# Up projection of a gated MLP: one pair of K tiles in seven block products, in 1024-column groups

## The chip, the cores and the metric

The kernel runs on one core of one Trainium2 chip. The metric is the device time of one execution in microseconds, the median of several runs of the same program. Beside it there is one profiled execution with its trace.

The engines are named as the profile names them: PE is TensorE (matmul; PEld its weight loads), DVE VectorE, ACT ScalarE, POOL GpSimd, SP the sequencer that issues nearly all transfers.

## The reference

One decoder layer on 256 tokens of width 2048: RMSNorm, a combined projection, mLSTM and forgetting-attention heads, an output projection with a residual, then the gated MLP, then a gated per-layer embedding. The part that matters here is the MLP:

```python
h = rms_norm(x, ffn_norm_g[i])
u = h @ w_up[i]                          # (256, 2048) @ (2048, 2 * 5632)
a, g = jnp.split(u, 2, axis=-1)
a = causal_dwconv(a, conv_w[i], conv_b[i])     # width 3, per column, over the tokens
x = x + (jax.nn.gelu(a, approximate=False) * g) @ w_down[i]
```

All of it is float32. The activations are only drawn from random inputs; sizes are fixed (`SEQ = 256`, `D_MODEL = 2048`, `D_FF = 5632`).

## The kernel before, in words

**Products.** Every large product is made in three matmuls of 128 x 128 by 128 x 512: weights and activations are split into a rounded part `hi` and a rest `lo`, and `hi*hi + hi*lo + lo*hi` is summed in PSUM. The activations are the stationary operand (128 features by 128 tokens) and the weights move. The 256 tokens are two halves, `t = 0, 1`.

**The stream of weights.** `run_stream` (L213) takes a list of steps. A step has weight sources of 512 KB (`srcs`), a `split` and a `fn`. SP loads a source into one of six `raw` buffers (four of `RAW`, two of `RAW_FFN`); a load is issued only once the buffer six loads earlier has been given back, strictly in order. `halves` (L200) splits a raw block: ScalarE casts it to `hi` (L208), VectorE subtracts to get `lo` (L210). There are five hi/lo pairs, and splits are issued four steps ahead of the matmuls: the loop issues the split of step i+4, then the matmuls of step i, and then pulls two pieces of work from side jobs (`pull`, L173).

**What sets the order.** This program order is a priority, not the final order. The tile framework plans the program on a timeline of its own, and on each engine an instruction that is ready there can pass an earlier one that still waits there. On the chip each engine then keeps the planned order.

**Up projection before.** `up(q)` (L1009) for q = 0 to 10 makes 512 columns of `a` and the 512 matching columns of `g`, each by `token_group` (L263): eight steps of two K tiles, twelve matmuls each, into two PSUM banks. At its end `up_evac` (L913) scales each bank on ScalarE into `z` (L918), and VectorE transposes it in 32 x 32 blocks into `sq` (L919). After the last bank the side job `ffn_job(q)` (L925) is queued: sixteen transfers `Y<-sq` (L931) on SP complete the transposition, then come the convolution (ScalarE L951, eight multiply-adds on VectorE L954, the halo on GpSimd), GELU (L962), the product with `g` (L966) and the split into `uT` (L129, L130). For the K pairs listed in `SEVEN`, four sums E3, E5, E6, E7 of the activation's blocks are made as well (L980) and split into `uE`.

**Down projection before.** After q = 5 and after q = 10 `down` (L1079) multiplies the finished part of `u` by `w_down`, in two groups of 1024 columns each, by `quad_group` (L303). A group has four banks D11, D21, D12, D22 (token half, column half). A K tile in plain form (kind "R", 12 matmuls) adds to all four. Some pairs of K tiles are done as a 2 x 2 block product in seven products instead of eight (Strassen, in Winograd's form): step "o1" (two raws loaded, one split whole, 6 matmuls), "o2" (half a raw split, then four adds of weight blocks in place in the two raws, L357; 3 matmuls), "c1" and "c2" (each raw split whole, 6 matmuls each). Three of the seven products go straight into D banks, four into further banks Q1, Q5, Q6 and Q7, so 21 matmuls take the place of 24. The raw buffers of o1 are given back only at c1 and c2. After the last c2 `mid` combines the Q banks; after a D bank's last matmul `end` takes it up. `weave` (L1022) writes the order out by hand: so many plain steps first (`head`), then per pair o1, n//3 plain steps, o2, the rest of n less one, c1, c2 and one more.

**PSUM.** Two tags, `mm` and `aux`, of four banks each. In a quad group the D banks have one and the Q banks the other, changed over from group to group.

Of the kernel before, what the change touches and what calls it, by code (L numbers as in the profile page):

```python
# [9 lines left out]
F32 = mybir.dt.float32  # L10
# [27 lines left out]
QF = 24  # L38
SEVEN = ((3, 5, 7), (13, 15, 17))
PAD = 112  # L40


@with_exitstack
def layer_kernel(
# [858 lines left out]
    with tc.tile_pool(name="ffn", bufs=1) as fp:  # L903
        uT = fp.tile([P, QF, 512], F32R, name="uT")
        uE = fp.tile([P, max(map(len, SEVEN)), 4, 256], F32R, name="uE")
# [5 lines left out]
        sq = {}  # L911

        def up_evac(q, ag):  # L913
            def f(t, b):
                if ag == 0 and t == 0:
                    sq[q] = fp.tile([P, 2, 4, NT, 4, 32], F32, tag="sq", name="sq")
                z = fp.tile([P, 512], F32, tag="z", name="z", bufs=3)
                act.activation(z, b, AF.Copy, scale=rstd2[:, t : t + 1])  # L918
                dve.transpose(sq[q][:, ag, :, t].rearrange("p j f r -> p f j r"),  # L919
                              z.rearrange("p (f j c) -> p f j c", f=4, j=4))  # L920
                if ag == 1 and t == NT - 1:
                    side.append(ffn_job(q))
            return f

        def ffn_job(q):  # L925
# [46 lines left out]
            for p in (2 * q, 2 * q + 1):  # L972
                if p in in_seven:
                    f = 2 * (p % 2)
                    v = u[:, f : f + 2].rearrange("p f t i r -> p f t (i r)")
                    e = cf[:, 0:512].rearrange("p (e s) -> p e s", e=4)
                    a11, a12, a21, a22 = v[:, 0, 0], v[:, 1, 0], v[:, 0, 1], v[:, 1, 1]
                    for dst, p0, p1 in ((e[:, 1], a21, a22), (e[:, 3], a21, a11), (e[:, 2], a11, e[:, 1]),
                                        (e[:, 0], a12, e[:, 2])):
                        dve.tensor_sub(dst, p0, p1)  # L980
                    yield
                    w = uE[:, in_seven[p]].rearrange("p u (e s) -> p u e s", e=2)
                    act.copy(w[:, :, 0], e)
                    dve.tensor_sub(w[:, :, 1], e, f32(w[:, :, 0]))
                    yield
# [20 lines left out]
        blocks = []  # L1006
        x2 = aT["cur"]

        def up(q):  # L1009
            for ag in range(2):  # L1010
                blocks.extend(token_group(w_up, all_k, lambda: x2, ag * FF + q * 512, 512, up_evac(q, ag),
                                          tag=("mm", "aux")[ag]))

        def u_unit(p, name):
            if name[0] == "E":
                v = uE[:, in_seven[p], "3567".index(name[1])]
                return v[:, 0:128], v[:, 128:256]
            t, i = int(name[0]) - 1, int(name[1]) - 1
            v = uT[:, (2 * p + i) % QF]
            return v[:, t * P : (t + 1) * P], v[:, 256 + t * P : 256 + (t + 1) * P]  # L1020
# [10 lines left out]

        def tmp(i):
            return fp.tile([P, 512], F32, tag="z", name=f"t{i}", bufs=3)

        pT = {}

        def load_p():
            pr = tmp(3).rearrange("p (t d) -> p t d", t=NT)
            nc.sync.dma_start(out=pr, in_=p[0, 0].rearrange("(t p) d -> p t d", p=P))
            yield 6  # L1040
# [4 lines left out]
            pT["t"] = fp.tile([P, 2, 512], F32R, tag="c", name="pT")  # L1045
            for k in range(2):
# [3 lines left out]
        def down_mid(c, ends):  # L1050
            def f(st):
                if ends and c == 0:
                    side.append(load_p())
                xc = [[xs[:, t, (c + n) * 512 : (c + n + 1) * 512] for n in range(2)] for t in range(NT)]
# [24 lines left out]
        def down(pairs, seven, ends, order):  # L1079
            for c in (0, 2):  # L1080
# [3 lines left out]
                cols = w_down[0][:, c * 512 : (c + 2) * 512].rearrange("k (h n) -> k h n", h=2)  # L1084
                tags = ("aux", "mm") if (c == 0) == ends else ("mm", "aux")
                grp = quad_group(lambda k, cols=cols: cols[k * P : (k + 1) * P], seq, u_unit, tags, down_mid(c, ends),
                                 down_end(c, ends))
                if c == 0:
                    st = grp[first]
                    st.fn = lambda hi, lo, fn=st.fn: (pull(10 ** 6), fn(hi, lo))  # L1090
                blocks.extend(grp)

        for q in range(6):
# [11 lines left out]
        def gate_done(c0, n):  # L1105
            sg = {}

            def f(t, b, i=0, j=n):
                if "r" not in r3:
                    r3["r"] = rstd_of(ssq3, "ple")  # L1110
                if i == 0:
                    sg[t] = fp.tile([P, 512], F32, tag="z", name="sg", bufs=3)
                w = (j - i) // (2 if i else 1)
# [46 lines left out]
```

## Time and profile before

| | us |
|---|---|
| median of 3 runs | 1254.61 (1253.37 to 1256.06) |
| profiled execution | 1254.04 |
| its span, first to last instruction | 1252.2 |
| PE busy | 1246.1 |
| DVE busy | 808.4 |
| ACT busy | 662.6 |
| mean granted TensorE clock | 1.000 |

The time of an execution holds 1.8 us outside the span. In the profile's groups, a row has the line, engine and operation, the tiles written and read, the shape and the count, then busy time in all, mean ns of one, idle time before them and what ended it. In a timeline row the first number is the start, the second the length, both in us, and the bracket has the engine's idle time before it and what ended it. The stage limits in the text (434.2, 697.2, 802.6, 1020.4, 1147.3 us from the span's start) are the first matmuls of up 0 to 5, the first down, up 6 to 10, the second down and the last stage.

### The profile page before, as it was taken

The page shows a single profiled execution, that of the slowest core. Times are in us where ns is not written, and L with a number is a line of the kernel's source. Part 1 is how long each engine was busy: PE and PEld are TensorE (multiplying, and loading weights), DVE is VectorE, ACT ScalarE, POOL GpSimd, SP SyncE. Part 2 cuts the span into 40 slices and gives each one's busy share as a digit, 9 for nine tenths or more (in the row PEclk, how much of TensorE's full clock was granted, in tenths as well). Part 3 has the DMA queues.
Part 4 walks back from the last instruction along what each step waited for, and adds up shares of the span by engine and source line. Part 5 has one row for each costly group of instructions (what it writes and reads, how often), then busy time and mean ns, then how long its engine had stood idle before and what let it go on. Part 6 is the DMA issues. An engine that isn't in the chain of part 4 may idle for free.

```text
span 1252.2 us, 16051 instructions
## 1 busy us (share of the span) xinstructions
PE 1246.1 (100%) x5699; PEld 1048.7 (84%) x5699; DVE 808.4 (65%) x1044; ACT 662.6 (53%) x918; POOL 35.8 (3%) x90
## 2 busy tenths in 40 slices
PE   9999999999999999999999999999999999999998
PEld 7899988888888888888888888888888888888887
DVE  6455566555565555676576697847577659978554
ACT  7555545445554555555465554445455546556542
POOL 2000000000000000000000000000000000000000
PEclk9999999999999999999999999999999999999999
DMA  8667877864567767677777675767767765787661
GB/s 286 173 180 219 255 237 216 209 180 137 162 185 196 236 222 218 202 224 218 212 223 226 186 241 169 234 190 215 231 200 230 222 193 185 222 217 247 205 210 51
DMA packets 161856, 258.77 MB, mean 207 GB/s; under 512 B 38377, under 2 KB 65905, under 8 KB 161777
## 3 DMA queue, kind: packets, MB, share of 16 engines
q1 hardware_dynamic: 161168, 257.57, 68.9%
q8 instruction: 44, 0.72, 0.2%
q14 instruction: 35, 0.29, 0.1%
q10 hardware_dynamic: 385, 0.16, 0.0%
q0 software_dynamic: 224, 0.03, 0.0%
HBM read 237.76 MB, written 2.12 MB: 192 GB/s over the span
## 4 chain that ended last, share of the span: by engine, by line
PE 99%; DMA 0%; SPq 0%; DVE 0%; ACT 0%; issue 0%; DVEq 0%
PE tg L288 26%; PE tg L289 26%; PE tg L290 26%; PE qgD L324 5%; PE qgD L325 5%; PE qgD L326 5%; PE qgQ L325 1%; PE qgQ L324 1%; PE qgQ L326 1%; PE xT L141 1%; PE mob L752 0%; DMA xs<-in_x_dram 0%; PE sc L633 0%; PE ob L661 0%; PE msc L727 0%; PE pt L654 0%
## 5 line engine op out<-in xcount | busy, mean ns | idle before, releaser
L210 DVE TENSOR_TENSOR lo<-raw,hi 128x1024 fp32r<-128x1024 f32 (+3 forms) x475 | 561.4, 1190 | 370.8 <-ACT hi L208 356.4
L208 ACT CAST hi<-raw 128x1024 fp32r<-128x1024 f32 (+3 forms) x475 | 482.6, 1025 | 455.1 <-PE tg L290 304.7
L288 PE MATMUL tg<-hi,x2T 128*128 128x512 f32 x704 | 274.1, 389 | 0.0
L290 PE MATMUL tg<-hi,x2T 128*128 128x512 f32 x704 | 274.0, 389 | 0.0
L289 PE MATMUL tg<-lo,x2T 128*128 128x512 f32 x704 | 273.9, 389 | 0.0
L288 PE MATMUL tg<-hi,hT 128*128 128x512 f32 (+2 forms) x480 | 181.8, 383 | 0.0
L289 PE MATMUL tg<-lo,hT 128*128 128x512 f32 (+2 forms) x480 | 180.3, 378 | 0.0
L290 PE MATMUL tg<-hi,hT 128*128 128x512 f32 (+2 forms) x480 | 180.2, 379 | 0.0
L289 PEld LDWEIGHTS tg<-lo,x2T 128*128 128x128 f32 x704 | 132.1, 188 | 27.5
L290 PEld LDWEIGHTS tg<-hi,x2T 128*128 128x128 f32 x704 | 132.1, 188 | 27.4
L288 PEld LDWEIGHTS tg<-hi,x2T 128*128 128x128 f32 x704 | 132.1, 188 | 27.3
L325 PE MATMUL qgD<-lo,uT 128*128 128x512 f32 x286 | 111.3, 389 | 0.0
L326 PE MATMUL qgD<-hi,uT 128*128 128x512 f32 x286 | 111.2, 389 | 0.0
L324 PE MATMUL qgD<-hi,uT 128*128 128x512 f32 x286 | 103.6, 389 | 0.0
L290 PEld LDWEIGHTS tg<-hi,hT 128*128 128x128 f32 x480 | 89.9, 188 | 12.7
L289 PEld LDWEIGHTS tg<-lo,hT 128*128 128x128 f32 x480 | 90.2, 188 | 12.2
L288 PEld LDWEIGHTS tg<-hi,hT 128*128 128x128 f32 x480 | 90.0, 188 | 12.0
L326 PEld LDWEIGHTS qgD<-hi,uT 128*128 128x128 f32 x286 | 53.7, 188 | 11.2
L324 PEld LDWEIGHTS qgD<-hi,uT 128*128 128x128 f32 x286 | 53.7, 188 | 11.2
L325 PEld LDWEIGHTS qgD<-lo,uT 128*128 128x128 f32 x286 | 53.7, 188 | 11.0
L289 PE MATMUL tg<-lo,x3T 128*128 128x512 f32 (+1 forms) x144 | 52.7, 366 | 0.0
L288 PE MATMUL tg<-hi,x3T 128*128 128x512 f32 (+1 forms) x144 | 52.7, 367 | 0.0
(227 smaller groups left out, 1093.3 us busy)
## 6 DMA issues: line engine op xcount, KB each, us to landing
raw<-in_w_up_dram SPq DMA_DIRECT2D x176, 512.0 KB, 4.6
raw<-in_w_down_dram SPq DMA_DIRECT2D x88, 512.0 KB, 4.7
raw<-in_w_in_dram SPq DMA_DIRECT2D x79, 512.0 KB, 4.3
raw<-in_w_out_dram SPq DMA_DIRECT2D x32, 512.0 KB, 4.3
raw<-in_w_ple_gate_dram SPq DMA_DIRECT2D x32, 512.0 KB, 4.7
Y<-sq SPq DMA_DIRECT2D x176, 64.0 KB, 3.2
raw<-in_w_in_dram SPq DMA_DIRECT2D x24, 416.0 KB, 3.6
raw<-in_w_in_dram SPq DMA_DIRECT2D x16, 408.0 KB, 3.7
```

Of the source, the lines that this page charges most:

```text
L141: pe.transpose(bk[:, t * P : (t + 1) * P], xs[:, t, k * P : (k + 1) * P], ident)
L208: act.copy(hi[:, :w], raw[:, :w])
L210: dve.tensor_sub(lo[:, :w], raw[:, :w], f32(hi[:, :w]))
L288: pe.matmul(bk[:, : e - c], ah, h[:, i, c:e], start=first, stop=False)
L289: pe.matmul(bk[:, : e - c], ah, l[:, i, c:e], start=False, stop=False)
L290: pe.matmul(bk[:, : e - c], al, h[:, i, c:e], start=False, stop=last)
L324: pe.matmul(st[bk], ah, hi[:, cols], start=first, stop=False)
L325: pe.matmul(st[bk], ah, lo[:, cols], start=False, stop=False)
L326: pe.matmul(st[bk], al, hi[:, cols], start=False, stop=final)
```

## The change

For q = 1 to 10 the two 512-column groups become one `quad_group` of 1024 columns (columns of `a` and of `g` are the two column halves), with D banks for token half and a/g. One K pair, pair 0 (`S_UP`), is done in seven products, the other seven pairs in plain form; the order is four plain steps, o1, one plain, o2, three plain, c1, c2 and six plain. Group 0 stays as it was. Pair 0's activation sums are made once, by the side job `x2_sums` in group 0, on VectorE, and split into `x2E`.

`up_mid` combines the Q banks into four SBUF tiles t11 to t22, scaled by the token's RMS factor: two reads of Q1 on ScalarE, four sums on VectorE, three scalings on ScalarE. `up_end` replaces the ScalarE evacuation of each bank by one VectorE instruction, bank x factor + tile, and the transposition follows as before.

Room is found elsewhere: the convolution's tile `c` now lies in the second half of `sq`, the E sums of the downs are kept in ten places (E3 of a pair takes the place of that pair's block 21, which seven products don't read; pair 7, which is also used in plain form, has its own), and four temporaries `t0` to `t3` replace the three buffers `z`. The second down's second group has five plain steps first instead of four, p is loaded at the start of the second down, and PSUM tags alternate through one counter.

```diff
+ONCE = (7,)
+S_UP = (0,)
+UP_ORDER = (4, (5,))
...
+        def x2_sums():
+            for i, p in enumerate(S_UP):
+                a = tmp(0).rearrange("p (k s) -> p k s", k=2)
+                e = tmp(1).rearrange("p (e s) -> p e s", e=4)
+                x = x2[:, 2 * p : 2 * p + 2, :]
+                dve.tensor_add(a, f32(x[:, :, 0:256]), f32(x[:, :, 256:512]))
+                a11, a12, a21, a22 = a[:, 0, 0:128], a[:, 1, 0:128], a[:, 0, 128:256], a[:, 1, 128:256]
+                for dst, p0, p1 in ((e[:, 1], a21, a22), (e[:, 3], a21, a11), (e[:, 2], a11, e[:, 1]),
+                                    (e[:, 0], a12, e[:, 2])):
+                    dve.tensor_sub(dst, p0, p1)
+                yield
+                h = x2E[:, i].rearrange("p u (e s) -> p u e s", e=2)
+                act.copy(h[:, :, 0], e)
+                dve.tensor_sub(h[:, :, 1], e, f32(h[:, :, 0]))
+                yield
...
+        def up_mid(q):
+            def f(st):
+                t11, t12, t21, t22 = (tmp(i) for i in range(4))
+                act.copy(t22, st["Q1"])
+                act.activation(t11, st["Q1"], AF.Copy, scale=rstd2[:, 0:1])
+                dve.tensor_sub(t21, st["Q6"], t22)
+                dve.tensor_add(t12, st["Q5"], t21)
+                dve.tensor_add(t21, st["Q7"], t21)
+                dve.tensor_add(t22, st["Q7"], t12)
+                for v, r in ((t12, rstd2[:, 0:1]), (t21, nr[:, 1:2]), (t22, rstd2[:, 1:2])):
+                    act.activation(v, v, AF.Copy, scale=r)
+                comb[q] = (t11, t12), (t21, t22)
+            return f
+
+        def up_end(q):
+            def f(t, ag, b):
...
+                z = comb[q][t][ag]
+                dve.scalar_tensor_tensor(out=z, in0=b, scalar=rstd2[:, t : t + 1], in1=z, op0=ALU.mult, op1=ALU.add)
+                dve.transpose(sq[q][:, ag, :, t].rearrange("p j f r -> p f j r"),
+                              z.rearrange("p (f j c) -> p f j c", f=4, j=4))
+                if ag == 1 and t == NT - 1:
+                    side.append(ffn_job(q))
+            return f
...
-            c = fp.tile([P, 4, NT, 4, 32], F32, tag="c", name="c")
+            c = T[:, 1].rearrange("p j t f r -> p (j t f r)").rearrange("p (i t f r) -> p i t f r", i=4, t=NT, f=4)
...
         def up(q):
-            for ag in range(2):
-                blocks.extend(token_group(w_up, all_k, lambda: x2, ag * FF + q * 512, 512, up_evac(q, ag),
-                                          tag=("mm", "aux")[ag]))
+            if q == 0:
+                for ag in range(2):
+                    blocks.extend(token_group(w_up, all_k, lambda: x2, ag * FF, 512, up_evac(q, ag),
+                                              tag=("aux", "mm")[ag]))
+                return
+            cols = w_up[0].rearrange("k (h n) -> k h n", h=2)[:, :, q * 512 : (q + 1) * 512]
+            seq = weave([p for p in range(KD // 2) if p not in S_UP], S_UP, *UP_ORDER)
+            blocks.extend(quad_group(lambda k: cols[k * P : (k + 1) * P], seq, x2_unit, tags(), up_mid(q), up_end(q)))
...
-        down(range(10, 22), SEVEN[1], True, ((6, (3, 2, 2)), (4, (3, 3, 3))))
+        down(range(10, 22), SEVEN[1], True, ((6, (3, 2, 2)), (5, (3, 3, 3))))
```

More of the change, by code (lines that the diff above doesn't have):

```diff
@@ new lines, in x2_unit @@
+        def x2_unit(p, name):
+            if name[0] == "E":
+                v = x2E[:, S_UP.index(p), "3567".index(name[1])]
+                return v[:, 0:128], v[:, 128:256]
+            t, k = int(name[0]) - 1, 2 * p + int(name[1]) - 1
+            return x2[:, k, t * P : (t + 1) * P], x2[:, k, 256 + t * P : 256 + (t + 1) * P]
+        nr = sm.tile([P, NT], F32, name="nr")
+        dve.tensor_scalar_mul(nr, rstd2, -1.0)
+        comb = {}
+        def up_mid(q):
[11 more added lines that the diff above has]
+            return f
@@ new lines, in up_end @@
+        def up_end(q):
+            def f(t, ag, b):
+                if t == 0 and ag == 0:
+                    sq[q] = fp.tile([P, 2, 4, NT, 4, 32], F32, tag="sq", name="sq")
+                z = comb[q][t][ag]
[5 more added lines that the diff above has]
+            return f
@@ L981, in ffn_job @@
                     yield
-                    w = uE[:, in_seven[p]].rearrange("p u (e s) -> p u e s", e=2)
-                    act.copy(w[:, :, 0], e)
-                    dve.tensor_sub(w[:, :, 1], e, f32(w[:, :, 0]))
+                    n = 3 * in_seven[p]
+                    w = uE[:, n : n + 3].rearrange("p u (e s) -> p u e s", e=2)
+                    v3 = uE[:, 9] if p in ONCE else uT[:, 2 * p % QF]
+                    v3 = v3.rearrange("p (e s) -> p e s", e=2)[:, :, -128:]
+                    act.copy(w[:, :, 0], e[:, 1:4])
+                    act.copy(v3[:, 0], e[:, 0])
+                    dve.tensor_sub(w[:, :, 1], e[:, 1:4], f32(w[:, :, 0]))
+                    dve.tensor_sub(v3[:, 1], e[:, 0], f32(v3[:, 0]))
                     yield
@@ L1006, in layer_kernel, with tags @@
         blocks = []
[L1007 removed]
+        turns = [0]
+        def tags():
+            turns[0] ^= 1
+            return ("aux", "mm") if turns[0] else ("mm", "aux")
         def up(q):
[L1010 to L1012 removed]
+            if q == 0:
[6 more added lines that the diff above has]
+            blocks.extend(quad_group(lambda k: cols[k * P : (k + 1) * P], seq, x2_unit, tags(), up_mid(q), up_end(q)))
         def u_unit(p, name):
[L1015 to L1016 removed]
+            if name in ("E5", "E6", "E7") or name == "E3" and p in ONCE:
+                v = uE[:, 9 if name == "E3" else 3 * in_seven[p] + "567".index(name[1])]
                 return v[:, 0:128], v[:, 128:256]
[L1018 removed]
+            t, i = (1, 0) if name == "E3" else (int(name[0]) - 1, int(name[1]) - 1)
             v = uT[:, (2 * p + i) % QF]
@@ L1039, in load_p @@
             nc.sync.dma_start(out=pr, in_=p[0, 0].rearrange("(t p) d -> p t d", p=P))
-            yield 6
+            while "bank" not in pT:
+                yield 1
             bk = bank("mm", "pTp")
@@ L1052, in f @@
                 if ends and c == 0:
-                    side.append(load_p())
+                    pT["bank"] = True
                 xc = [[xs[:, t, (c + n) * 512 : (c + n + 1) * 512] for n in range(2)] for t in range(NT)]
@@ L1084, in down @@
                 cols = w_down[0][:, c * 512 : (c + 2) * 512].rearrange("k (h n) -> k h n", h=2)
-                tags = ("aux", "mm") if (c == 0) == ends else ("mm", "aux")
-                grp = quad_group(lambda k, cols=cols: cols[k * P : (k + 1) * P], seq, u_unit, tags, down_mid(c, ends),
+                grp = quad_group(lambda k, cols=cols: cols[k * P : (k + 1) * P], seq, u_unit, tags(), down_mid(c, ends),
                                  down_end(c, ends))
@@ L1090, in down @@
                     st.fn = lambda hi, lo, fn=st.fn: (pull(10 ** 6), fn(hi, lo))
+                    if ends:
+                        grp[0].fn = lambda hi, lo, fn=grp[0].fn: (fn(hi, lo), side.append(load_p()))
                 blocks.extend(grp)
+        side.append(x2_sums())
         for q in range(6):
```

14 lines of the change are left out of this document (8 added, 6 removed).

## The prediction

> **What bounds the kernel now.** I read the page first (busy times, slices, chain), then the waits, then busy time by stage.
>
> ```profile
> span 1252.2 us, 16051 instructions
> PE 1246.1 (100%) x5699; PEld 1048.7 (84%) x5699; DVE 808.4 (65%) x1044; ACT 662.6 (53%) x918; POOL 35.8 (3%) x90
> DVE  6455566555565555676576697847577659978554
> ...
> PE 99%; DMA 0%; SPq 0%; DVE 0%; ACT 0%; issue 0%; DVEq 0%
> ```
>
> TensorE is the whole chain. A busy PE need not be a dense one, so the waits of PE and the distance between starts of matmuls decide (first the waits, then PE's timeline, where the two rows are twelve matmuls apart):
>
> ```profile
> PE warm L81 <- DVE ones L77: 1.1, 1, 1.1
> PE xT L141 <- DMA xs<-in_x_dram: 0.8, 1, 0.8
> ...
> DVE lo L210 <- ACT hi L208: 356.4, 287, 4.6
> ACT hi L208 <- PE tg L290: 304.7, 208, 2.4
> ACT c L951 <- DMA Y<-sq: 19.4, 11, 3.3
> ```
>
> ```profile
> 802.62 0.39 PE L288 MATMUL tg<-hi,x2T 128*128 128x512 f32 x1
> ...
> 805.34 0.39 PE L288 MATMUL tg<-hi,x2T 128*128 128x512 f32 x1
> ```
>
> PE waits 1.9 us in all, both at the start; a 512-column matmul costs 2.72 / 12 = 0.2267 us. ScalarE waits for PE to give back hi/lo buffers and VectorE waits for ScalarE: both follow PE. By stage (up 0-5, first down, up 6-10, second down, then two dense Strassen stretches of the downs):
>
> ```profile
> core 0: us, PE busy (x) PEld busy (x) DVE busy (x) ACT busy (x) POOL busy (x), PEclk, DMA share, GB/s
> 434.20:697.20 263.00, 263.00 (x1169) 217.74 (x1168) 168.51 (x217) 142.61 (x166) 8.32 (x28) 1.00 0.73 219
> 697.20:802.60 105.40, 105.40 (x466) 87.28 (x465) 88.23 (x106) 55.30 (x59) 2.14 (x5) 1.00 0.65 208
> 802.60:1020.40 217.80, 217.80 (x962) 180.35 (x961) 138.42 (x175) 112.92 (x126) 5.93 (x20) 1.00 0.72 214
> 1020.40:1147.30 126.90, 126.90 (x563) 105.02 (x563) 107.78 (x135) 70.74 (x88) 2.08 (x5) 1.00 0.70 211
> 719.00:748.00 29.00, 29.00 (x130) 24.01 (x128) 27.35 (x33) 16.64 (x18) 0.00 (x0) 1.00 0.73 248
> 1046.70:1069.80 23.10, 23.10 (x103) 19.12 (x103) 21.71 (x24) 13.25 (x15) 0.00 (x0) 1.00 0.59 191
> ```
>
> The downs already use seven products for some pairs, in the same code that the change uses for the up projection. The first down has 465 matmuls by the code, and 465 x 0.2267 = 105.4 us, its whole length: nothing is lost there, with VectorE busy 88.23 / 105.40 = 84%, and 94% in the two dense stretches. The clock is 1.00 throughout.
>
> **The change part by part.**
>
> *TensorE, on the path.* A pair of K tiles costs a 1024-column group 24 matmuls in four-product form (2 K tiles x 4 banks x 3) and 21 in seven products. One pair in ten groups: 30 matmuls less, 30 x 0.2267 = **-6.80 us**. A group falls from 192 to 189 matmuls, 42.85 us. Nothing else leaves the path.
>
> The page "TensorE: Matmul & The Clock Gate" of the Trainium skill (section "Wait — 56ns, not 53.3ns?") gives a warm 512-column matmul 215.7 ns from start to start; by it the saving would be 6.5 us. The trace has 226.7 ns for this kernel's matmuls, and the sum goes by the trace.
>
> *VectorE and ScalarE, beside the path.* Prices (groups by form):
>
> ```profile
> L210 DVE TENSOR_TENSOR lo<-raw,hi 128x1024 fp32r<-128x1024 f32 x422 | 513.0, 1221 | 321.0 <-ACT hi L208 306.7 <-DMA Y<-sq 7.5 <-DMA raw<-in_w_in_dram 5.2
> L208 ACT CAST hi<-raw 128x1024 fp32r<-128x1024 f32 x422 | 440.2, 1051 | 414.5 <-PE tg L290 278.4 <-PE qgD L326 47.9 <-DVE raw L357 18.2
> L919 DVE STREAM_TRANSPOSE sq<-z 128x512 f32<-128x512 f32 x44 | 31.1, 707 | 6.6 <-ACT z L918 6.6
> L918 ACT ACTIVATE z<-tg,rstd_ffn 128x512 f32<-128x512 f32 x44 | 30.2, 685 | 14.2 <-PE tg L290 14.2
> L951 ACT ACTIVATE c<-Y,cT 128x256 f32<-128x256 f32 x44 | 22.9, 591 | 19.4 <-DMA Y<-sq 19.4
> L954 DVE SCALAR_TENSOR_TENSOR c<-Y,cT,c 128x248 f32<-128x248 f32 x44 | 20.8, 475 | 11.7 <-ACT c L951 11.5
> L357 DVE TENSOR_TENSOR raw<-raw,raw 128x512 f32<-128x512 f32 x22 | 15.2, 691 | 0.6
> L962 ACT ACTIVATE c<-c 128x1024 f32<-128x1024 f32 x11 | 11.7, 1061 | 3.7 <-DVE c L960 3.6
> L210 DVE TENSOR_TENSOR lo<-raw,hi 128x512 fp32r<-128x512 f32 x13 | 9.0, 693 | 7.5 <-ACT hi L208 7.4
> L208 ACT CAST hi<-raw 128x512 fp32r<-128x512 f32 x13 | 8.1, 621 | 10.9 <-PE qgD L326 5.0 <-DMA raw<-in_w_in_dram 3.2 <-DVE lo L210 1.7
> L1076 DVE TENSOR_TENSOR xs<-qgD,xs 128x512 f32<-128x512 f32 x8 | 5.3, 681 | 1.1 <-PE qgD L326 1.1
> L133 DVE SCALAR_TENSOR_TENSOR x2T<-xT,vT,x2T 128x256 fp32r<-128x256 f32 x8 | 3.5, 477 | 0.6 <-ACT x2T L132 0.6
> L1059 DVE TENSOR_TENSOR t<-qgQ,t 128x512 f32<-128x512 f32 x4 | 2.7, 686 | 0.0
> L1056 ACT COPY t<-qgQ 128x512 f32<-128x512 f32 x4 | 2.3, 574 | 0.0
> ```
>
> VectorE, per group: the Strassen pair is split three times whole and once half instead of twice whole, 1.22 + 0.69, and its weight sums are four adds, 4 x 0.69: +4.67. The middle (Q banks) is four sums, 4 x 0.686: +2.74. The end is four scalar_tensor_tensor of 512 columns with one operand in PSUM, which the trace lacks: not below the plain add's 0.68 (L1076), not above two of 256 columns, 0.95 (L133). I take 0.74, nearer the plain add, since length sets most of it: +2.96. Together +10.4 on 138.42 / 5 = 27.7, so **38.1 of 42.85 us, 89%**. ScalarE loses four evacuations (4 x 0.685) and gets one and a half casts (1.05 + 0.62), a copy and a scaled read of PSUM (0.57 + 0.69) and three scalings out of SBUF of 512 columns, between 0.59 and 1.06 (L951, L962), say 0.75: +2.4 on 22.6, 25.0 of 42.85. All this is priced at nothing on the path; what hides it is the stock of split blocks ahead of PE. With that cover gone each microsecond of VectorE over 42.85 would cost ten, once per group. The dense rows' 94% would carry 38.1 in 40.5 us.
>
> The sums of x2 once, in group 0, some 5 us of VectorE, and the E sums of the downs in four instructions instead of two, lie under the same cover; nothing there.
>
> *The stock, step by step.* There are five hi/lo pairs, so block i+4 is split when PE has finished block i-1, some 10.9 us before its turn (ScalarE's and VectorE's timelines):
>
> ```profile
> 854.50 1.05 ACT L208 CAST hi<-raw 128x1024 fp32r<-128x1024 f32 x1 [1.67 <-PE tg L290]
> ...
> 855.59 1.23 DVE L210 TENSOR_TENSOR lo<-raw,hi 128x1024 fp32r<-128x1024 f32 x1 [1.50 <-ACT hi L208]
> ```
>
> It is done 2.3 us later, so 8.6 us in stock. Let T be the moment PE finishes a group. In the new order (four plain blocks, o1, plain, o2, three plain, c1, c2, six plain) PE starts o1 at T+10.9, o2 at 15.0, c1 at 23.8, c2 at 25.2 and the plain block behind (number 12) at 26.5. VectorE's end is four times 0.74 + 0.71, with one lo between; the first bank closes nine matmuls before T, so from T-1.9 to T+5.1. Behind it stand o1, a plain lo, o2 with its four adds and two more lo: done at 6.3, 7.5, 11.0, 12.2, 13.4, needed at 10.9, 12.2, 15.0 (o2's matmuls), 15.6, 18.4. Smallest stock 3.4 us.
>
> *Two queues the end is moved past.* The sixteen transposing DMAs of the finished group wait at SP for the last transpose. Before (SP, ScalarE):
>
> ```profile
> 847.85 2.51 SPq L931 DMA_DIRECT2D Y<-sq  x4
> ...
> 858.15 2.50 SPq L931 DMA_DIRECT2D Y<-sq  x4
> ...
> 863.34 2.08 ACT L951 ACTIVATE c<-Y,cT 128x256 f32<-128x256 f32 x4 [2.34 <-DMA Y<-sq]
> ```
>
> Group 6 ended at 802.62 + 192 x 0.2267 = 846.1, so Y was there at T+17.2. Afterwards the issue starts at T+5.1 and not T+1.7, but no weight load stands between, since o1 gives no buffer back: 16 x 0.625 = 10 us, plus the 2.7 us that lay between the last issue (860.65) and the landing: T+17.8, say 18. The wait is in ScalarE's queue: behind the convolution (L951) stand the casts, behind these the lo subtractions. GpSimd, 3% busy, waits for the same Y and has nothing else queued.
>
> c1's lo gives back the raw buffer into which SP loads block 12, and every later load is behind that one. The downs have this chain (VectorE: two lo, the first is c1's, ending at 760.98; ScalarE):
>
> ```profile
> 759.75 2.58 DVE L210 TENSOR_TENSOR lo<-raw,hi 128x1024 fp32r<-128x1024 f32 x2 [0.94 <-ACT hi L208]
> ...
> 764.72 1.05 ACT L208 CAST hi<-raw 128x1024 fp32r<-128x1024 f32 x1 [0.92 <-DMA raw<-in_w_down_dram]
> ```
>
> From the end of c1's lo to the dependent cast: 3.74 us. c1's hi/lo buffers come free at T+15.0. If it is split then, its lo ends at T+17.4, block 12 could be cast at 21.2, and VectorE, behind eight multiply-adds (8 x 0.475, from 18.6 to 22.4), has its lo at T+23.6: 3 us in stock. Cost nothing.
>
> *Where I chose.* The planner orders by its own timeline. Before, the convolution stands behind block 9's cast and ahead of block 10's (ready at T+16.3), and ScalarE then waited 19.4 / 11 = 1.8 us: the planner believes Y some 2 us early. With Y at T+18 on the chip it plans some T+16, later than T+15.0, so c1's cast goes ahead. That is my forecast: -6.80 and no new stall. The profiled execution took 1254.04 us, its span 1252.2 and 1.8 around it; 1254.04 - 6.80 = 1247.24. The median of the runs, 1254.61, is 0.57 above the profiled one: **1247.8 us**.
>
> **Rivals.**
>
> *Convolution ahead of c1 (slower).* If the planner has Y before T+15.0, ScalarE stands until 18. In the rows above the cast after the convolution began 2.0 us behind its start, and VectorE's lo, between the multiply-adds, ends some 4.7 behind it: c1's lo at T+22.7, block 12 cast at 26.4, lo done at 28.7, needed 26.75. PE stalls 1.9 us per group, 19 us in all: 1266.8. It decides from a c1 lo later than T+20.7; with half the groups so, 1257. For it: ScalarE waited on Y in all eleven groups. Against: the planner knows the later issue.
>
> *VectorE as the bound.* The page "Perfetto Trace Analysis" of the Trainium skill (section "Identifying the Most-Contended Engine") judges VectorE by its busy share and TensorE by its weight loads' share; 38.1 / 42.85 is 89% against PEld's 83%, so by it VectorE becomes the engine that limits the up stage. Worked from rows: VectorE idles about 2 us before c1 and again wherever a lo waits for its cast. At an effective 87.5% a group takes 43.5 us, 0.68 us more than PE's, and the gain is gone: 1254.6. At the downs' mean of 84.5% (196.01 / 232.30) it would be 45.1 us and 1270. Against: the dense rows show 94% at an undelayed PE.
>
> *Loss in the downs.* Groups 5 and 10 end inside a down, whose raw loads now stand at SP behind the later Y issues (T+5.1), and the convolution comes 2 us later among three Strassen pairs, where VectorE already has 94%. One to three us, once or twice: 1250.
>
> *Nothing saved* would need the matmuls to be back in number; the code has none.
>
> **How the numbers follow.** Forecast 0.52; loss in the downs 0.13; VectorE as the bound near balance 0.16; convolution ahead of c1, in half or all groups, 0.16; other losses 0.03. What this kernel's measurement can tell from no change is about 0.2%, 2.5 us, so from 1252.1 to 1257.1 is the same. Faster: 0.52 + 0.13 + 0.02 of the third = 0.67; same: 0.12; slower: 0.21. Alone, the forecast ranges from 1246.3 (the runs shown lie up to 1.45 us from their median) to 1250; to leave out no more than 2 in 10 the range goes to 1262, with the light form of the first rival.
>
> **What would show it.** PE records fall by 30 to 5669; PE still waits about 2 us in all; in up 6-10 the five groups take 214.2 us and VectorE is busy 190; ScalarE's c1 cast stands ahead of the convolution. Wrong would be: gaps of PE ahead of block 12, waits of casts for in_w_up, or VectorE above 95% in the up stages with PE waiting for lo.

## The result and the profile after

The changed kernel takes **1247.49 us** (median of six runs, 1247.33 to 1248.62) where the kernel before takes 1254.26 us on the same chip (six runs, 1253.37 to 1256.06). The ratio is 0.9946, 95% interval 0.9934 to 0.9959: faster by 0.54%. The forecast was 1247.8. The profiled execution took 1247.99 us, with a span of 1246.2 instead of 1252.2.

The page of the changed kernel (busy times, then the chain that ended last), and the two rows of TensorE in its waits:

```profile
span 1246.2 us, 16204 instructions
...
PE 1240.2 (100%) x5669; PEld 1043.4 (84%) x5669; DVE 900.9 (72%) x1197; ACT 681.8 (55%) x955; POOL 41.7 (3%) x90
...
PE 95%; DMA 2%; DVE 1%; SPq 1%; issue 1%; ACT 0%; DVEq 0%; ACTq 0%
```

```profile
PE warm L84 <- DVE ones L80: 1.1, 1, 1.1
PE qgD L327 <- ACT hi L211: 0.6, 2, 0.4
```

There are 30 matmuls less, 5699 to 5669. TensorE still waits for almost nothing, but a new wait has come: 0.6 us for a cast, which the kernel before didn't have.

Busy time by stage of the changed kernel: up groups 1 to 5, first down, then up groups 6, 7, 8, 6 to 10 together, and the second down (columns as in the prediction's stage table):

```profile
479.14:693.34 214.20, 214.20 (x947) 177.43 (x945) 184.22 (x254) 128.56 (x153) 9.47 (x25) 1.00 0.68 222
693.34:798.74 105.40, 105.40 (x467) 87.30 (x465) 90.94 (x112) 54.34 (x58) 2.65 (x5) 1.00 0.63 207
798.74:841.58 42.84, 42.84 (x191) 35.48 (x189) 29.47 (x33) 21.26 (x23) 0.00 (x0) 1.00 0.65 201
841.58:884.42 42.84, 42.84 (x191) 35.48 (x189) 38.11 (x56) 25.54 (x31) 1.76 (x5) 1.00 0.67 218
884.42:927.26 42.84, 42.84 (x191) 35.48 (x189) 37.65 (x55) 25.56 (x31) 2.52 (x5) 1.00 0.68 214
798.74:1012.94 214.20, 214.20 (x947) 177.42 (x945) 180.11 (x243) 122.92 (x145) 8.11 (x20) 1.00 0.67 218
1012.94:1141.00 128.06, 127.44 (x563) 104.92 (x562) 110.96 (x141) 70.20 (x87) 3.21 (x5) 1.00 0.66 211
```

Five groups take 214.20 us, which is 945 x 0.2267: no matmul of the ten changed groups waits. The first down takes its 105.40 again. Only the second down is longer, 128.06 against 126.90. So the span's difference of 6.0 is made up of -6.80 (30 matmuls), +1.16 (second down), -0.53 (the first matmul of up 0 stands at 433.67 instead of 434.20), and some 0.2 that isn't placed.

**A group's chain on the chip.** Group 6 ends at T = 841.58. VectorE, SP and ScalarE in group 7:

```profile
842.83 1.37 DVE L968 SCALAR_TENSOR_TENSOR t<-qgD,rstd_ffn,t 128x512 f32<-128x512 f32 x2
...
845.84 1.29 DVE L969 STREAM_TRANSPOSE sq<-t 128x512 f32<-128x512 f32 x2
...
847.21 11.09 SPq L993 DMA_DIRECT2D Y<-sq  x16
...
856.78 2.00 ACT L211 CAST hi<-raw 128x1024 fp32r<-128x1024 f32 x2 [1.71 <-PE qgD L329]
...
859.76 2.09 ACT L1013 ACTIVATE sq<-Y,cT 128x256 f32<-128x256 f32 x4
...
862.60 1.05 ACT L211 CAST hi<-raw 128x1024 fp32r<-128x1024 f32 x1 [0.75 <-DMA raw<-in_w_up_dram]
```

The last transpose is done at 847.13 = T+5.5. The sixteen issues last to T+16.7. The casts of c1 and c2 begin at T+15.2 and stand ahead of the convolution (L1013), which begins at T+18.2 and waits for nothing.

**The loss in the second down.** ScalarE of the changed kernel around 1112, then ScalarE of the kernel before at the same work:

```profile
1112.38 3.31 ACT L877 ACTIVATE x3T<-turnY,vT 128x256 fp32r<-128x256 f32 x8 [3.04 <-DMA turnY<-turnT]
1115.60 3.45 ACT L211 CAST hi<-raw 128x1024 fp32r<-128x1024 f32 x4
```

```profile
1115.88 1.05 ACT L208 CAST hi<-raw 128x1024 fp32r<-128x1024 f32 x1 [2.20 <-DMA raw<-in_w_down_dram]
1116.83 3.30 ACT L874 ACTIVATE x3T<-turnY,vT 128x256 fp32r<-128x256 f32 x8
```

Before, a cast went ahead of the eight x3T evacuations. Now the evacuations come first, wait 3.04 us for their transposing transfers, and four casts stand behind them. Two matmuls begin 0.58 and 0.38 us late right there (after 1115.88 and 1117.03).

### The profile page after: what moved, and what is told of

It reads as the page before. It is cut to its first block, busy times and chain, and to the rows that moved or that the text cites. A ratio compares the mean times of both kernels' runs of the same rounds, so it can differ in the third digit from the quotient of the medians.

```text
span 1246.2 us, 16204 instructions
## 1 busy us (share of the span) xinstructions
PE 1240.2 (100%) x5669; PEld 1043.4 (84%) x5669; DVE 900.9 (72%) x1197; ACT 681.8 (55%) x955; POOL 41.7 (3%) x90
## 4 chain that ended last, share of the span: by engine, by line
PE 95%; DMA 2%; DVE 1%; SPq 1%; issue 1%; ACT 0%; DVEq 0%; ACTq 0%
PE qgD L327 15%; PE qgD L329 15%; PE qgD L328 15%; PE tg L291 14%; PE tg L293 14%; PE tg L292 14%; PE qgQ L329 1%; PE qgQ L327 1%; PE qgQ L328 1%; DMA raw<-in_w_down_dram 1%; SPq L870 1%; PE xT L144 1%; DVE lo L213 1%; PE mob L755 0%; DMA xs<-in_x_dram 0%
## 5 line engine op out<-in xcount | busy, mean ns | idle before, releaser
L213 DVE TENSOR_TENSOR lo<-raw,hi 128x1024 fp32r<-128x1024 f32 (+3 forms) x495 | 577.9, 1180 | 270.9 <-ACT hi L211 261.7
L211 ACT CAST hi<-raw 128x1024 fp32r<-128x1024 f32 (+3 forms) x495 | 498.1, 1017 | 454.9 <-PE qgD L329 183.4
L328 PE MATMUL qgD<-lo,x2T 128*128 128x512 f32 x580 | 225.6, 389 | 0.0
L329 PE MATMUL qgD<-hi,x2T 128*128 128x512 f32 x580 | 225.6, 389 | 0.0
L327 PE MATMUL qgD<-hi,x2T 128*128 128x512 f32 x580 | 217.5, 389 | 0.0
L329 PEld LDWEIGHTS qgD<-hi,x2T 128*128 128x128 f32 x580 | 108.9, 188 | 22.6
L327 PEld LDWEIGHTS qgD<-hi,x2T 128*128 128x128 f32 x580 | 108.9, 188 | 22.6
L328 PEld LDWEIGHTS qgD<-lo,x2T 128*128 128x128 f32 x580 | 108.9, 188 | 22.5
L329 PE MATMUL qgD<-hi,uT 128*128 128x512 f32 x296 | 115.2, 389 | 0.0
L328 PE MATMUL qgD<-lo,uT 128*128 128x512 f32 x296 | 115.2, 389 | 0.0
L327 PE MATMUL qgD<-hi,uT 128*128 128x512 f32 x296 | 104.0, 390 | 0.6 <-ACT hi L211 0.6
L327 PEld LDWEIGHTS qgD<-hi,uT 128*128 128x128 f32 x296 | 55.4, 188 | 12.8 <-ACT hi L211 1.5
L329 PEld LDWEIGHTS qgD<-hi,uT 128*128 128x128 f32 x296 | 55.6, 188 | 11.6
```

Source lines behind the costliest of these rows:

```text
L211: act.copy(hi[:, :w], raw[:, :w])
L213: dve.tensor_sub(lo[:, :w], raw[:, :w], f32(hi[:, :w]))
L327: pe.matmul(st[bk], ah, hi[:, cols], start=first, stop=False)
L328: pe.matmul(st[bk], ah, lo[:, cols], start=False, stop=False)
L329: pe.matmul(st[bk], al, hi[:, cols], start=False, stop=final)
```

## The experiments

Each edit is shown against the changed kernel. Every kernel was timed against the kernel before on the same chip; the ratios go by that one.

**The new grouping without seven products.** The groups have 1024 columns in four banks, but all eight pairs are plain, and ScalarE evacuates.

```diff
-            seq = weave([p for p in range(KD // 2) if p not in S_UP], S_UP, *UP_ORDER)
-            blocks.extend(quad_group(..., seq, x2_unit, tags(), up_mid(q), up_end(q)))
+            seq = [("R", k) for k in range(KD)]
+            blocks.extend(quad_group(..., seq, x2_unit, tags(), None, up_plain(q)))
```

> All the groups of the up projection stay 1024 columns wide (four D banks per group, changed tags, c in the second half of sq), but every K pair is in plain form: 192 matmuls per group again, no weight sums, no middle, and the ends are scaled by ScalarE as before. If the time follows the number of matmuls alone: 1247.5 + 30 x 0.2267 = 1254.3, the time of before within 0.2%. If the wider groups bring or cost something of their own, it is off 1254.3 by more than 2.5 us; a gain of the regrouping itself would show as 1250 or so.

Measured: 1255.37 us, ratio 1.0008 (0.9999 to 1.0018). The regrouping by itself brings nothing. It already has a loss in the second down, of 1.9 us by the length of that stage: one matmul there is 1.42 us late, and some smaller delays follow it.

**Seven products in the odd groups alone.** Groups 2, 4, 6, 8 and 10 get the plain sequence above.

```diff
+            if q % 2 == 0:
+                seq = [("R", k) for k in range(KD)]
+                blocks.extend(quad_group(..., None, up_plain(q)))
+                return
```

> Seven products for pair 0 in the five odd groups only, the five even groups wide and plain. By the number of matmuls half of the gain: 1247.5 + 15 x 0.2267 = 1250.9. If VectorE already took something back in the full version, half the groups keep more than half of the gain, below 1250.

Measured: 1251.53 us, ratio 0.9983 (0.9974 to 0.9992), so 2.5 us of the 3.4 expected from fifteen matmuls. The plain groups take 43.52 us and the others 42.84, as by the matmuls. In the second down of the profiled execution 0.86 us is lost, which with the 2.5 makes up the 3.4. (That execution itself took 1253.26 us: its up projection also began 1.7 us later than that of the kernel before, in code that no run changes.)

**The c1 cast behind the convolution.** The split of c1 is tied to the last instruction of the convolution that was traced before it.

```diff
+                def split(_, step=opened[p]):
+                    if unit.__name__ == "x2_unit" and "conv" in last:
+                        with tc.issue_after(last["conv"]):
+                            return halves(step.raws[0], BLK)
+                    return halves(step.raws[0], BLK)
...
+                last["conv"] = traced()
```

> The changed kernel with one more rule for the planner: in the up groups c1's cast stays behind the convolution on ScalarE, so it waits for Y too. My chain: the convolution starts 18.2 us after the group's end, c1's cast 2 us later, its lo ends 4.7 us behind the convolution's start, the next plain block is cast 3.5 us after that and is 1.9 us late. Eight groups have a convolution of that kind (not 1, whose Y is early, and not 6, whose job ran in the down): 8 x 1.9 = 15 us, 1262.7. The rival, that stock or the planner absorbs it: below 1250.

Measured: 1254.78 us, ratio 1.0005 (0.9996 to 1.0014): 7 us slower than the changed kernel, half of what was expected. The tie took hold in groups 3, 4, 8 and 9 only; in the others c1's split had been traced ahead of the convolution. Of these four, two lost time (group 3 by stage, then ScalarE in it):

```profile
564.85:610.69 45.84, 43.74 (x191) 35.25 (x189) 38.62 (x56) 25.53 (x31) 1.26 (x5) 1.00 0.66 210
```

```profile
582.91 2.09 ACT L1017 ACTIVATE sq<-Y,cT 128x256 f32<-128x256 f32 x4 [1.04 <-DMA Y<-sq]
584.90 2.00 ACT L211 CAST hi<-raw 128x1024 fp32r<-128x1024 f32 x2
...
591.77 1.04 ACT L211 CAST hi<-raw 128x1024 fp32r<-128x1024 f32 x1 [2.53 <-DMA raw<-in_w_up_dram]
```

The casts of c1 and c2 come 2.0 us after the convolution's start, as the rival had it, and block 12's cast then waits for its load. Group 3 lost 3.0 us, group 8 (887.45 to 933.33) the same; groups 4 and 9 took 42.84 us and lost nothing, since block 12's cast found its load there. The theory formed from this: of the six raw buffers four are in one class and two in another, and block 12 has to wait for c1's lo only where pair 0's two blocks lie in the class of two. A group has 16 loads, so its place in the ring of six moves by four, and only some groups are hit.

**The same, with the ring turned by two.**

```diff
-                if nl % ring < RAW:
+                if (nl + 2 * (ring > RAW)) % ring < RAW:
```

> The run with the c1 cast behind the convolution, with the order of the load buffers turned by two, so that the first pair's blocks of a group fall into the two-buffer class in groups 1, 4, 6 and 9 instead of 3 and 8. Theory (the load of block 12 waits for c1's lo part only there): TensorE's losses of 2.9 us move from groups 3 and 8 to 4 and 9, and the time is about 1254.8 again, within 2. Rival (something else about groups 3 and 8): the losses stay in groups 3 and 8, at the same time. Third: with more than one of these groups hit, more is lost, up to 1260.

Measured: 1259.94 us, ratio 1.0041 (1.0026 to 1.0055). Groups 3 and 8 are back at 42.84 us. Groups 4 and 9 by stage:

```profile
609.02:655.96 46.94, 44.58 (x191) 36.48 (x189) 38.35 (x56) 25.61 (x31) 1.26 (x5) 0.96 0.69 217
932.72:979.85 47.13, 44.74 (x191) 36.53 (x190) 38.58 (x56) 25.52 (x31) 1.26 (x5) 0.96 0.69 220
```

The losses have moved from groups 3 and 8 to 4 and 9, as the ring theory had it, and the rival (something else about groups 3 and 8) is out. The size was off: 4.1 and 4.3 us instead of 3.0 a group, since here the clock fell behind the stall (0.96 as the mean of the group, last section). The rest of the 5 us over the run before it (2.8 us) is mostly in the second down, which loses some 3.5 us instead of 1.7.

**VectorE loaded further.** Four, then eight adds of 128 x 512 per group, written in `up_mid`, whose results nobody uses; they only add work.

```diff
+                for _ in range(4):          # 8 in the second run
+                    junk = sm.tile([P, 512], F32, tag="junk", name="junk")
+                    xe = f32(x2E[:, 0].rearrange("p u s -> p (u s)"))
+                    dve.tensor_add(junk, xe[:, 0:512], xe[:, 512:1024])
```

> Four additional VectorE adds of 512 columns behind each group's middle, results unused: 4 x 0.69 = 2.8 us more VectorE per group, from some 36.4 to 39.2 of 42.84, 91%. If VectorE is under the cover of the stock: 1247.5, within 1 us. If VectorE were the bound of the up stage already, each microsecond would cost ten: 1275.

> Eight additional VectorE adds of 512 columns behind each group's middle: 5.5 us more, 41.9 of 42.84, 98%. VectorE also has waits of its own, so here the cover should give out: at the 94% of the dense stretches of the downs a group takes 44.6 us, 1.7 us more, ten times 1.7, some 1264. If idle time of VectorE counts for nothing: 1247.5 still.

Measured: 1249.54 us, ratio 0.996 (0.9948 to 0.9972), and 1258.74 us, ratio 1.0032 (1.0019 to 1.0045). Neither loaded all ten groups. The adds depend on nothing of their group, and the planner moved them into groups 0 and 1 (25 and 15 of the 40) and into groups 0 to 4. What they do show is what a nearly full VectorE costs there (group 1 with four; groups 1, 2 and 3 with eight):

```profile
481.00:523.84 42.84, 42.84 (x191) 35.47 (x190) 41.42 (x60) 26.87 (x31) 5.62 (x5) 1.00 0.71 219
```

```profile
478.75:521.59 42.84, 42.84 (x190) 35.47 (x189) 42.05 (x61) 26.86 (x31) 5.72 (x5) 1.00 0.70 214
521.59:564.68 43.09, 43.09 (x190) 35.39 (x189) 42.09 (x61) 24.69 (x29) 3.86 (x5) 1.00 0.68 210
564.68:617.00 52.32, 44.92 (x191) 36.29 (x189) 51.71 (x80) 26.32 (x34) 1.16 (x5) 0.93 0.59 180
```

VectorE busy for 97% and 98% of group 1 costs nothing, and in group 2 0.25 us. Group 1 is a light one, though (33.50 us of VectorE work in the changed kernel), filled up with adds that wait for nothing. In group 3 there is more work than an undelayed group is long, 51.71 us of it, and TensorE waits; group 4 loses another 1.7 us. Group 3 doesn't tell a want of VectorE time from a late end of the group before: its last transpose is done at T+16.7 instead of T+5.5, and ScalarE waits 5.71 us for Y with the next casts behind. With four adds no group loses more than 0.1 us; of the 2 us over the changed kernel, the profiled execution has 1.8 ahead of the first matmul of up 0.

**Eight adds tied to the middle of their own group.** They read what the middle has made.

```diff
+                for _ in range(8):
+                    junk = sm.tile([P, 512], F32, tag="junk", name="junk")
+                    dve.tensor_add(junk, t12, t21)
```

> Eight adds of 128x512 whose results nobody uses, behind each group's middle and reading what the middle made, so that they can't be moved to another group. The rows of the changed kernel give VectorE 36.0 to 36.8 us in a group of 42.84; eight more, at 0.64 to 0.69 us each, make 41.1 to 42.3, or 96 to 99%. If VectorE's queue bounds nothing until it is full: 1247.5 to 1250. If it binds from 94 to 95% on because its waits can't all be filled (the rival of VectorE as the bound): each of ten groups takes 1 to 2 us more, 1257 to 1268.

Measured: 1279.28 us, ratio 1.0189 (1.0172 to 1.0206), over every case. My sum for the load was wrong: it went by 36.0 to 36.8 us per group, means that include light groups. A full group has 37.7 (mean of the stage rows of groups 2 to 5 and 7 to 10), and eight adds at 0.61 us from start to start make 42.6, or 99.4%. And the adds did not stay in their group. Group 2's eight ran from 560.3 to 575.4, across its end at T = 565.01. By stage, groups 3 and 10; then VectorE, SP, ScalarE and TensorE in group 3, and the convolution in group 10:

```profile
565.01:616.97 51.96, 45.31 (x191) 36.90 (x190) 46.00 (x69) 25.51 (x31) 1.37 (x5) 0.93 0.62 188
994.35:1037.19 42.84, 42.84 (x190) 35.47 (x189) 39.98 (x55) 22.32 (x27) 2.69 (x5) 1.00 0.64 189
```

```profile
580.14 1.29 DVE L972 STREAM_TRANSPOSE sq<-t 128x512 f32<-128x512 f32 x2
...
591.05 0.69 DVE L954 TENSOR_TENSOR t<-qgQ,t 128x512 f32<-128x512 f32 x1 [5.51 <-PE qgQ L329]
...
581.50 10.30 SPq L996 DMA_DIRECT2D Y<-sq  x16
...
593.45 2.08 ACT L1016 ACTIVATE sq<-Y,cT 128x256 f32<-128x256 f32 x4 [9.16 <-DMA Y<-sq]
...
597.27 2.93 ACT L211 CAST hi<-raw 128x1024 fp32r<-128x1024 f32 x3
...
598.35 2.08 PE L327 MATMUL qgD<-hi,x2T 128*128 128x512 f32 x4 [6.65 <-ACT hi L211]
...
1030.60 2.08 ACT L1016 ACTIVATE sq<-Y,cT 128x256 f32<-128x256 f32 x4 [2.24 <-DMA Y<-sq]
```

The last transpose of the group's end, done at T+5.5 in the changed kernel, is done here at 581.4 = T+16.4, because the adds and the splits stand ahead of it. Y is issued to T+26.8, the convolution waits 9.16 us for it on ScalarE, the next casts stand behind the convolution, and TensorE stands 6.65 us for block 12. Meanwhile VectorE itself is idle for 5.51 us. So the stall is a late end of the group, not a want of VectorE time at that moment. Groups 3, 5 and 8, in which 13 or 14 adds ran, lost 9.1, 6.3 and 8.7 us; the other seven lost nothing, and the second down takes some 7 us more than in the changed kernel, which wasn't looked into.

A late end alone isn't enough, as group 10 of the same run shows (T = 994.35). It held 13 adds, and its last transpose was done later still, at 1017.83 = T+23.5. But here the convolution stands behind the next casts in ScalarE's order, at T+36.3, and the group took 42.84 us. So by this contrast the stall needs both, a late end and a convolution that stands ahead of the casts. No edit separates the two, and group 10 is followed by the down.

**Two pairs in seven products per group.** The places for E sums go to a second up pair, and the downs have two pairs in each group; by matmuls alone 1242.7 us. First with one plain step after the last c2:

```diff
-SEVEN = ((3, 5, 7), (13, 15, 17))
-S_UP = (0,)
-UP_ORDER = (4, (5,))
+SEVEN = ((3, 5), (13, 15))
+S_UP = (0, 1)
+UP_ORDER = (4, (4, 4))
```

> Two pairs (0 and 1) in seven products in each of the ten groups; to find the room, the downs do only two pairs each (3, 5 and 13, 15). Matmuls: 30 less in up, 9 more in the downs, -21 x 0.2267 = -4.8: 1242.7 by their number. VectorE gets 4.7 us more per group, some 41 of 42.16, 97%. If the bound is VectorE above 94 to 95%, each group takes 43.5, and the time is 1256; if the planner can fill VectorE, 1243.

Measured: 1287.58 us, ratio 1.0253 (1.0227 to 1.028). Groups 1 and 6 take 42.16 us, the others 43.2 to 50.0, with VectorE busy for 85 to 90% of them. At the end of its group 7 (T = 903.07) the combination of the Q banks stands among the end's instructions, and SP's issue and the convolution come late:

```profile
912.89 1.29 DVE L969 STREAM_TRANSPOSE sq<-t 128x512 f32<-128x512 f32 x2
...
925.99 2.08 ACT L1013 ACTIVATE sq<-Y,cT 128x256 f32<-128x256 f32 x4 [3.59 <-DMA Y<-sq]
```

The last transpose is done at T+11.1 instead of T+5.5. I took this late middle for the cause. The same kernel with the weight sums of the up pairs on GpSimd:

```diff
-                        dve.tensor_add(dst, dst, oth)
+                        (pool if unit.__name__ == "x2_unit" else dve).tensor_add(dst, dst, oth)
```

> As with two pairs, but the four adds of weight blocks per pair run on GpSimd in the up groups: VectorE is 5.5 us lower, 35.5 of 42.16. If VectorE was the bound with two pairs, this comes to 1243; if GpSimd's adds of 512 columns, which no trace shows, take longer than the 2 us each that lie between o1 and c1, or hold VectorE up, it is slower than with the adds on VectorE.

Measured: 1310.47 us, ratio 1.0447 (1.0429 to 1.0464), slower still. GpSimd takes 1.64 and 2.18 us for an add that takes VectorE 0.69 (groups of GpSimd in this run), and the casts behind wait for them, 78.8 us in all:

```profile
L360 POOL TENSOR_TENSOR raw<-raw 128x512 f32<-128x512 f32 x40 | 87.2, 2181 | 397.1 <-DVE lo L213 395.6
L360 POOL TENSOR_TENSOR raw<-raw,raw 128x512 f32<-128x512 f32 x40 | 65.8, 1644 | 3.1
```

**Two pairs, with four plain steps after the last c2**, to take the late middle away:

```diff
-UP_ORDER = (4, (4, 4))
+UP_ORDER = (3, (3, 3))
```

> Two pairs in seven products in each group, as in the run with two pairs, but with four plain steps behind the last of the c2 casts instead of one, and the downs as in the kernel before's order of two pairs there. By the matmuls alone 1242.7. Theory (the late middle was what cost the run with two pairs its time): VectorE works some 40.7 us in a group of 42.16 and the time is 1243 to 1252. Rival (two pairs ask too much of VectorE or of the loads wherever they stand): it stays over 1270.

Measured: 1292.98 us, ratio 1.0297 (1.0275 to 1.032). My theory of the late middle has fallen: with the middle earlier the time is no better, and it is the rival's time, over 1270, that came. The groups take 42.2 to 49.9 us again, but they now lose it at another place, at the second pair. Group 3 by stage, and ScalarE in it (T = 574.44):

```profile
574.44:624.34 49.90, 46.43 (x187) 36.14 (x186) 42.56 (x62) 26.96 (x33) 1.26 (x5) 0.93 0.63 197
```

```profile
592.30 2.08 ACT L1013 ACTIVATE sq<-Y,cT 128x256 f32<-128x256 f32 x4 [4.33 <-DMA Y<-sq]
595.23 3.47 ACT L211 CAST hi<-raw 128x1024 fp32r<-128x1024 f32 x4 [0.84 <-DMA raw<-in_w_up_dram]
...
608.25 2.94 ACT L211 CAST hi<-raw 128x1024 fp32r<-128x1024 f32 x3 [1.85 <-DVE raw L360]
```

The second pair's chain (cast, weight sums, cast) now runs between the convolution's steps on the same two engines: casts wait for the weight sums (L360) and for loads, and the convolution itself waits 4.33 us for Y. So one of the two pairs meets either the convolution or the group's end. That this collision alone is the cause is read from the rows and was not isolated: VectorE needs 97% of such a group too (41.0 of 42.16, mean of groups 2 to 5), and which of the two decides, or whether the loads do, stays open. Not all of the loss is in the groups named: group 10 and the second down together take 9.2 us more in the run with one plain step than they would without a wait, and 13.3 in this one; where was not looked into.

**The second down's last group with four instead of five plain steps**, and its pairs spread wider, against the loss there:

```diff
-        down(range(10, 22), SEVEN[1], True, ((6, (3, 2, 2)), (5, (3, 3, 3))))
+        down(range(10, 22), SEVEN[1], True, ((6, (3, 2, 2)), (4, (4, 4, 4))))
```

> The changed kernel with another order in the second down's last group: four plain steps first and four instead of three plain steps from pair to pair. In the changed kernel PE lost 1.2 us there, at the third pair, with the stock down to nothing. One more plain step per pair gives VectorE 2.7 us each time: no loss, 1246.3. If the loss is not of the stock, 1247.5.

Measured: 1257.07 us, ratio 1.0017 (1.0008 to 1.0026), 11 us over what was expected. The reason I had for the loss, that the order there leaves too small a stock, doesn't lead to the cure. ScalarE in this run:

```profile
1113.94 1.71 ACT L877 ACTIVATE x3T<-turnY,vT 128x256 fp32r<-128x256 f32 x4 [3.27 <-DMA turnY<-turnT]
...
1120.72 4.41 ACT L211 CAST hi<-raw 128x1024 fp32r<-128x1024 f32 x5 [2.47 <-DMA raw<-in_w_down_dram]
```

The x3T evacuations wait as before, the next cast comes later still, and TensorE loses 3.47 us at 1118, then 2.97 us after 1145.66, where the middle of the last pair stands too near the end of the group. The matmuls behind these two waits run at half their pace for a while (last section), which costs some 2.9 and 1.3 us more.

**Two pairs in each group of the downs, one in the up groups.** Nine matmuls more than in the changed kernel, 2.04 us.

```diff
-SEVEN = ((3, 5, 7), (13, 15, 17))
-ONCE = (7,)
+SEVEN = ((3, 5), (13, 15))
+ONCE = ()
-        down(range(10, 22), SEVEN[1], True, ((6, (3, 2, 2)), (5, (3, 3, 3))))
+        down(range(10, 22), SEVEN[1], True, ((6, (3, 3)), (6, (3, 3))))
```

> The changed kernel with two instead of three pairs in the downs' second groups and in both of the second down: 9 matmuls more, +2.0 us, 1249.5; the second down's last group, where the changed kernel lost 1.2 us of PE time, has only two pairs in a row and should lose nothing: 1248.3. It is the base of the two runs with two pairs.

Measured: 1249.11 us, ratio 0.9961 (0.9946 to 0.9976). The chain is TensorE's again and no matmul between 1050 and 1140 is late:

```profile
PE 99%; DMA 0%; SPq 0%; DVE 0%; ACT 0%; issue 0%; DVEq 0%
```

So the loss in the second down goes with the third pair in its last group. The x3T evacuations wait for their transfers in this run too (1.19 us, with three casts behind them), and TensorE loses nothing. The removal of the loss is worth less than the nine matmuls cost.

## Why the prediction was right

**TensorE on the path: right.** -6.80 us, and both runs of five groups measure 945 x 0.2267. The half change bears out the price per group: 43.52 against 42.84.

**VectorE per group: 38.1 was met by luck; the increase was sized too high.** Groups 7 and 8 have 38.11 and 37.65 where 38.1 was predicted. But the prediction added its 10.4 us to 27.7, a mean of five groups with the light group 6 among them. A full group had 28.9 before (group 7):

```profile
846.14:889.66 43.52, 43.52 (x193) 36.04 (x192) 28.90 (x40) 23.51 (x27) 1.37 (x5) 1.00 0.74 218
```

So a full group gained some 9 us instead of 10.4, and a base that was too low made up for it. The five groups together have 180.1 instead of 190: they gained 8.3 us each. There are two reasons. Group 6 follows the down and carries no end of a group before it, so it gained only 5.6 (23.86 to 29.47). And instructions that follow each other without a wait overlap: the rows above have two scalar_tensor_tensor in 1.37 and two transposes in 1.29 us, and the 68 instructions that the five groups gained cost 41.7 us, 0.61 each, where my prices of single instructions mean 0.74. The unknown price, the scalar_tensor_tensor with a PSUM operand, was 0.735 (0.74 taken). ScalarE has 25.5 in these groups, and 24.6 as the mean of the five, where 25.0 was predicted.

**Two queues, and c1 ahead of the convolution: right.** Transposes done at T+5.5 (5.1), c1's cast at T+15.2 (15.0), convolution at T+18.2 (18).

**Block 12 waits for c1's lo: right in the groups that the ring hits, not in all.** The stock of 3 us is 4.1 in group 7 (block 12's lo is done at 864.91, the first matmul that reads it starts at 869.00), but as a rule for each group the step was too strict. The runs with c1 behind the convolution show the chain itself (load, cast and stall in the order the rival gave) in two of the four groups where c1 was late, and with the ring turned in the two others. So this rival's price was real, though the planner did not choose that order: with c1 held back it costs 3.0 us for each group hit instead of 1.9, or 4.2 with the fall of the clock, and for two of the ten groups instead of all; with it the gain is gone.

**VectorE as the bound: did not come.** It would have cost the gain at an effective 87.5%; in the loaded runs the light group 1 was dense at 97 and 98%, and the full group 2 lost 0.25 us at 98%. (196.01 / 232.30 is 84.4% and not 84.5%, which changes nothing.) The Trainium skill's page "Perfetto Trace Analysis" (section "Identifying the Most-Contended Engine") would call VectorE the most contended engine at 89%, against 83% of TensorE's weight loads; by it the up groups would now go at VectorE's pace, and the traces differ: 42.84 us, TensorE's pace exactly. The tied adds show what can decide before the capacity: where added work stands ahead of a group's end, Y comes late, and if the convolution then stands ahead of the next casts, the stall comes with VectorE idle.

**Loss in the downs: came, in a small form.** The forecast had no loss there; this rival had 1 to 3 us once or twice, by the later Y issues and the convolution among the pairs. It is 1.16 us, in the second down alone, and by another mechanism than the rival gave: ScalarE stands behind the x3T evacuations. The regrouping without seven products has such a loss too (1.9), so the seven products of the up groups don't bring it, and the run without the third pair in the downs hasn't. Which part of the regrouping brings it (the order of the last group with five plain steps first, the earlier load of p, the other PSUM tags) no run separates.

**The sum.** -6.80 from the profiled 1254.04 gave 1247.24; the profiled execution took 1247.99, 0.75 more, mostly by this loss less the 0.53 by which the MLP starts earlier. The earlier start is chance: the first matmul of up 0 stands anywhere between 433.19 and 436.57 in the profiled executions of all the runs, with nothing changed ahead of it. The medians differ by 6.77, which hides the loss; that they come so near to 6.80 is in part luck.

## What to carry to other kernels

Where an engine off the path is to get more work, price the full groups, not a stage's mean, and look first at what stands behind the work in that engine's order: VectorE at 98% cost next to nothing in two groups, and adds ahead of a group's end cost up to 9 us in a group where the convolution stood ahead of the next casts, and nothing where it stood behind them. A saving on the path comes through whole only as long as the next group's loads and casts stand ahead of every instruction that waits for a late transfer. A second helping of the same saving is a new question: two pairs per group would have saved 4.8 us more by the matmuls and cost 40 instead.

## What the runs showed of the hardware

**TensorE's clock falls behind a stretch of 3.41 us in which it did too little.** TensorE in group 4 of the run with the ring turned, then busy time and granted clock (the column ahead of the DMA share) in two stretches of it:

```profile
638.07 2.08 PE L327 MATMUL qgD<-hi,x2T 128*128 128x512 f32 x4 [2.36 <-ACT hi L211]
639.95 0.63 PE L328 MATMUL qgD<-lo,x2T 128*128 128x512 f32 x1
640.37 0.63 PE L329 MATMUL qgD<-hi,x2T 128*128 128x512 f32 x1
```

```profile
634.33:637.74 3.41, 1.39 (x7) 0.79 (x5) 3.14 (x7) 1.46 (x2) 0.00 (x0) 1.00 0.81 258
637.74:641.15 3.41, 3.08 (x7) 2.51 (x8) 3.10 (x5) 3.12 (x4) 0.00 (x0) 0.50 0.77 238
```

After 2.36 us of idleness the matmuls begin 0.42 to 0.43 us apart for some 3 us and are back at 0.227 at 641.2. That adds 1.5 us to the stall and is why a group hit there cost 4.2 us. In group 3 of the run with the unturned ring the longest wait was 1.34 us, and the matmuls kept their pace. But the length of the wait alone doesn't decide. In the second run with two pairs TensorE waited longer and kept its pace at full clock:

```profile
981.57 1.19 PE L327 MATMUL qgD<-hi,x2T 128*128 128x512 f32 x4 [3.07 <-ACT hi L211]
```

```profile
976.72:980.13 3.41, 1.78 (x8) 1.13 (x6) 1.82 (x5) 2.07 (x4) 1.04 (x4) 1.00 0.75 219
```

In the clock records of the traces every fall behind such a wait lasts 3.41 or 6.83 us, and within a run the falls begin whole multiples of 3.41 us apart (95 of them between the two in the run with the ring turned). Laid on that grid, from 40 us on and at full clock, each of the 19 stretches in which TensorE was busy for at most 0.45 of the time was followed by a fall, and none with 0.51 or more was; in between both occur. In the rows above the shares are 1.39 / 3.41 = 0.41, with a fall, and 1.78 / 3.41 = 0.52, without one: the wait of 3.07 us lies across two stretches. So what a stall of 2 to 3 us costs depends on how it falls on the grid.

The Trainium skill's page "TensorE: Matmul & The Clock Gate" (table in its part 1, "The HAM clock gate (the "warmup" mystery)") puts the fall to the slow state behind an idle window of about 3.4 us. The length agrees with the 3.41 here, but the window was not idle throughout in this trace: TensorE was busy for 1.39 us of it. The page's 426.7 ns for a cold 512-column matmul (section "Wait — 56ns, not 53.3ns?") agrees with the 0.42 to 0.43 us here.

**GpSimd beside a busy VectorE** took 1.64 to 2.18 us for an add of 128 x 512 that VectorE does in 0.69. What it takes beside an idle VectorE no run shows.
